# The same two-layer decoder with its long-lived SBUF tiles at other addresses

## The chip, the cores and the metric

The kernel runs on one core of a Trainium2 chip. The metric is the device time of one execution in microseconds (us); a lower time is better. The time before is the median of three runs, 2254.27 us (2254.26 to 2255.32).

## The reference, cut to what matters

Two layers over 256 tokens of width 2048, all in fp32. Layer 0 mixes tokens with forgetting attention (16 heads of 128), layer 1 with sliding-window attention (32 query heads, 4 key heads of 64, with sinks and rotary positions). Each mixer is followed by a gated feed-forward part of width 5632 with a causal convolution of width 3. Shift, scale and gate of every sub-layer come from a conditioning vector `c`.

```python
for i in range(DEPTH):
    mod = c_act @ ada_w[i] + ada_b[i]
    sh1, sc1, g1, sh2, sc2, g2 = jnp.split(mod[:, None, :], 6, axis=-1)
    h = x * (1.0 + sc1) + sh1
    y = fox_attention(h, ...) if i % 2 == 0 else swa_attention(h, ...)
    x = layer_norm(DEEPNORM_ALPHA * x + (1.0 + g1) * y, ln_mix_g[i], ln_mix_b[i])
    h = x * (1.0 + sc2) + sh2
    u = causal_conv3(h @ w_up) + conv_b
    y = (silu(u[..., :D_FF]) * u[..., D_FF:]) @ w_down
    x = layer_norm(DEEPNORM_ALPHA * x + (1.0 + g2) * y, ln_ffn_g[i], ln_ffn_b[i])
```

Weights dominate: about 600 MB of fp32 are read once from HBM.

## The kernel before, in words

**Arithmetic.** To keep fp32 precision with fast matmuls, every operand is split into a high and a low part of type fp32r, and a product is made of three: high times high, high times low, low times high. ScalarE casts a weight tile `w` to its high part `wh` (L276), VectorE subtracts to get the low part `wl` (L287). All matmuls go through the helper `mm`, so they all carry line 76.

**A step.** `stream` (L268) loads a weight tile of two 128-row blocks by 512 columns (512 KB), and one step uses it. There are three kinds of step.

- `w_stationary` (L342), the up-projection of the feed-forward part: the weights are stationary. Eight matmuls have a 128x128 block of `wh` stationary and stream 512 columns of `hHL` past it (high and low halves of the input, side by side); then eight have a block of `wl` stationary and stream the 256 columns of the high half. Their outputs are called `wd`, and the four blocks of 128 features go round four PSUM banks. 16 matmuls a step.
- `x_mm` (L298), with the input stationary: 128x128 blocks of the input stay, and 512 columns of `wh` or `wl` stream past. The input is `hHL` (fox values, all projections of layer 1; outputs `xs`), `gT` (the down-projection) or `oT` (the attention output). 12 matmuls a step, each of 512 columns. In the output projection the first 12 of the 16 blocks of `oT` lie in tiles of the pool `gp`; the last four are put into `hHL`, which is free by then (`o_tile`, L727).
- `w_mm` (L325), for query and key of layer 0 (outputs `ws`): weights stationary, 256 columns of `hHL` streaming. 24 matmuls a step.

**Order.** SP issues the loads, ten weight tiles ahead; `wh` and `wl` have four buffers each, so ScalarE and VectorE prepare up to four steps ahead of TensorE. Beside this VectorE sums the conditioning matrix row by row into `acc` (L406, `ada_vector`), paced by rates that were set by hand for each stage; transposes of `x` for the next modulation (L469, L508) and the short matmuls that turn `acc` into columns (output `sm`) are slipped in between two steps. `hHL` is written once for each sub-layer by `mod_pair` (L473). `gate` holds the row that scales a sub-layer's output (L621).

**Addresses.** A tile is a range of bytes that is the same in each partition. The pool `cst`, with one buffer for each name, lays its tiles out in the order in which the program first asks for them, each rounded up to 32 bytes, from byte 1152. The pools `wp` (`w`), `hl` (`wh`, `wl`) and `gp` (`gT`, `oT`, `qT` and others) follow; `wp` begins at byte 77312, which is 151 x 512, and all tiles of these three pools begin at multiples of 512 bytes. A [128, 24] tile named `gap`, 96 bytes that nothing uses, fills up `cst` to that point.

Of the kernel before, what the change touches and what calls it, by code (L numbers as in the profile page):

```python
# [10 lines left out]
F32 = mybir.dt.float32  # L11
F32R = mybir.dt.float32r
# [5 lines left out]
P = 128  # L18
D = 2048
S = 256  # L20
NT = S // P
KC = D // P
DEPTH = 2
FH = 16
FW = 2048
SQ = 32
# [15 lines left out]
def hybrid_trunk(ctx: ExitStack, tc: tile.TileContext, a: dict, out: bass.AP):  # L42
# [6 lines left out]
    cst = ctx.enter_context(tc.tile_pool(name="cst", bufs=1))  # L49
# [16 lines left out]
    def bank(name="sm"):  # L66
        return psp.tile([P, 512], F32, tag="ps", name=name)
# [10 lines left out]
    def pin(ins, on=True):  # L78

        if on:  # L80
            tc.keep_in_program_order(ins)
# [14 lines left out]
    adab = a["ada_b"].rearrange("l (r p) -> l r p", p=P)  # L96
    nc.sync.dma_start(rows0[:NADA, 1, :], adab[0])

    ident = cst.tile([P, P], F32, name="ident")
    nc.gpsimd.memset(ident, 0.0)  # L100
    nc.gpsimd.affine_select(out=ident, in_=ident, compare_op=ALU.not_equal, fill=1.0, base=0,
# [2 lines left out]
    nc.gpsimd.memset(ones, 1.0)  # L104

    mask = cst.tile([P, 3, P], F32, name="mask")
    nc.gpsimd.memset(mask, 0.0)
    nc.gpsimd.affine_select(out=mask[:, 1, :], in_=mask[:, 1, :], compare_op=ALU.is_gt, fill=NEG, base=0,
                            pattern=[[1, P]], channel_multiplier=-1)
    nc.gpsimd.affine_select(out=mask[:, 2, :], in_=mask[:, 2, :], compare_op=ALU.is_ge, fill=NEG, base=0,  # L110
                            pattern=[[-1, P]], channel_multiplier=1)

    sel = cst.tile([P, 2, FH], F32, name="sel")
    nc.gpsimd.memset(sel, 0.0)
    for j, bases in enumerate(((64, 96), (0, 32))):
        for b in bases:
            nc.gpsimd.affine_select(out=sel[:, j, :], in_=sel[:, j, :], compare_op=ALU.not_equal,
                                    fill=1.0, base=-b, pattern=[[-1, FH]], channel_multiplier=1)

    x = cst.tile([P, NT, D], F32, name="x")  # L120
    csil = cst.tile([KC, P], F32, name="csil")
    nc.scalar.activation(csil, rows0[:KC, 0, :], AF.Silu)
    cact = cst.tile([P, KC], F32, name="cact")
# [9 lines left out]
    HR = ROPE_DIM // 2  # L133
    lcol = cst.tile([P, 4, DEPTH, KC], F32, name="lcol")
    ccol = cst.tile([P, DEPTH, CW + 1, NF], F32, name="ccol")
    sink = cst.tile([P, SQ], F32, name="sink")
    nsink = cst.tile([P, SQ], F32, name="nsink")
    sint = cst.tile([P, NT, HR], F32, name="sint")
    cost = cst.tile([P, NT, HR], F32, name="cost")

# [29 lines left out]
    def rotary():  # L170

        nc.gpsimd.dma_start(sink, a["swa_sinks"][0].partition_broadcast(P))
        posr = cst.tile([NT, P], I32, name="posr")
        nc.gpsimd.dma_start(posr, a["positions"].rearrange("b (t p) -> (b t) p", p=P))
        yield
        pin(nc.vector.tensor_scalar_mul(nsink, sink, -1.0))
        posf = cst.tile([NT, P], F32, name="posf")
        pin(nc.vector.tensor_copy(posf, posr))
        yield
        pt = bank()  # L180
        nc.tensor.transpose(pt[:, :NT], posf, ident[:NT, :NT])
        yield
        posc = cst.tile([P, NT], F32, name="posc")
        nc.vector.tensor_copy(posc, pt[:, :NT])
        inv = [float(np.float32(ROPE_THETA ** (-2.0 * i / ROPE_DIM))) for i in range(HR)]
        ang = cst.tile([P, NT, HR], F32, name="ang")
        for i in range(HR):
            nc.vector.tensor_scalar_mul(ang[:, :, i], posc, inv[i])
        nturn = cst.tile([P, NT, HR], F32, name="nturn")
        nint = cst.tile([P, NT, HR], I32, name="nint")  # L190
        nc.vector.tensor_scalar_mul(nturn, ang, 1.0 / (2.0 * math.pi))
        nc.vector.tensor_copy(nint, nturn)
        nc.vector.tensor_copy(nturn, nint)
        c1 = 6.28125
        c2 = float(np.float32(np.floor((2 * math.pi - c1) * 2 ** 21) / 2 ** 21))
        c3 = 2 * math.pi - c1 - c2
        for cc in (c1, c2, c3):
            nc.vector.scalar_tensor_tensor(ang, nturn, -cc, ang, op0=ALU.mult, op1=ALU.add)
        PI = float(np.nextafter(np.float32(math.pi), np.float32(0)))
        nc.vector.tensor_scalar(ang, ang, PI, -PI, op0=ALU.min, op1=ALU.max)  # L200
        nc.vector.scalar_tensor_tensor(nturn, ang, -1.0, ang, op0=ALU.mult, op1=ALU.max)
        nc.vector.tensor_scalar(nturn, nturn, -1.0, 0.5 * math.pi, op0=ALU.mult, op1=ALU.add)
        yield
        nc.scalar.activation(sint, ang, AF.Sin)
        nc.scalar.activation(cost, nturn, AF.Sin)
# [249 lines left out]
            print("caught up", l, v, n)  # L455


    hHL = cst.tile([P, KC, 2, S], F32R, name="hHL")
    hH, hL = hHL[:, :, 0, :], hHL[:, :, 1, :]
    cst.tile([P, 24], F32, name="gap")  # L460

    def mod_turn(k, n=1):

# [298 lines left out]
    def fox(l, j):  # L762
# [156 lines left out]
        settle()  # L919
        forget_split()  # L920
        later([forget(), columns(), rotary(), scaled()])
        for blk, rate in zip(range(4), (1.0, 1.3, 1.5, 1.6)):
            then(lambda rate=rate: ada.update(rate=rate))
# [252 lines left out]
```

## Time and profile before

| | |
|---|---|
| median of three runs | 2254.27 us |
| the profiled execution's own time | 2256.26 us |
| its span, first to last instruction | 2254.5 us |
| TensorE busy (PE) | 2203.2 us, 98% |
| weight loads (PEld) | 1892.9 us, 84% |
| VectorE busy (DVE) | 1852.2 us, 82% |
| ScalarE busy (ACT) | 1193.7 us, 53% |
| granted TensorE clock, mean | 0.996 |

PE counts a matmul from its start to a modelled end, and matmuls overlap, so a PE that is busy all the time may still start its matmuls at a faster or slower rhythm. The rhythm can be read from the timeline, where matmuls of one kind are merged into a row with the time of the first start and their count: the start of the next row, less the start of this one, divided by the count, is the distance from one matmul to the next.

### The profile page before, as it was taken

The numbers are of one execution on the slowest core, as the hardware profiler recorded it, in microseconds if no ns is written. First come the engines' busy times: TensorE is split into PE (matmuls) and PEld (weight loads), VectorE is DVE, ScalarE is ACT, GpSimd is POOL, SyncE is SP. The second block draws the span as 40 slices with busy tenths as digits, with TensorE's granted clock in tenths as the row PEclk, the third lists the DMA queues.
The fourth block names the chain that finished last, engine by engine and source line by source line (L and its number), as shares of the span: only waits on it lengthen the run. The fifth ranks groups of instructions, "written<-read, shape, count | busy, mean of one in ns | idle before, by whom it ended". The sixth has DMA issues, their size and how long they took to land. (4 is left out here: it accounts for less than half of the span.)

```text
span 2254.5 us, 33348 instructions
## 1 busy us (share of the span) xinstructions
PE 2203.2 (98%) x12196; PEld 1892.9 (84%) x12196; DVE 1852.2 (82%) x2685; ACT 1193.7 (53%) x1873; POOL 19.9 (1%) x51
## 2 busy tenths in 40 slices
PE   7999999999999999999999999999999999999997
PEld 6988898788888888888887788888888888888886
DVE  7989998889988968978978989889988655676766
ACT  4546544356555433555534578646655533555542
POOL 0000000000000000000000000000000000000000
PEclk9999999999999999999999999999999999999999
DMA  9999999869978889878887867678887556666553
GB/s 345 393 372 311 341 379 355 305 222 307 313 243 273 316 292 333 287 226 285 280 307 261 288 202 262 219 254 290 285 268 242 187 194 190 190 192 189 189 194 111
DMA packets 287285, 602.68 MB, mean 267 GB/s; under 512 B 21830, under 2 KB 55304, under 8 KB 286608
## 3 DMA queue, kind: packets, MB, share of 16 engines
q1 hardware_dynamic: 286064, 595.86, 77.8%
q0 software_dynamic: 1056, 4.69, 0.6%
q8 instruction: 95, 1.56, 0.3%
q14 instruction: 70, 0.57, 0.1%
HBM read 598.37 MB, written 2.10 MB: 266 GB/s over the span
## 5 line engine op out<-in xcount | busy, mean ns | idle before, releaser
L276 ACT CAST wh<-w 128x1024 fp32r<-128x1024 f32 x728 | 764.7, 1051 | 802.0 <-PE wd L76 267.5
L287 DVE TENSOR_TENSOR wl<-w,wh 128x1024 fp32r<-128x1024 f32 x728 | 887.0, 1221 | 297.0 <-ACT wh L276 283.7
L76 PE MATMUL wd<-hHL,wh 128*128 128x512 f32 x2816 | 717.9, 397 | 1.1 <-DVE hHL L482 1.1
L76 PEld LDWEIGHTS wd<-hHL,wh 128*128 128x128 f32 x2816 | 503.4, 188 | 100.1 <-issue 2.9
L76 PEld LDWEIGHTS wd<-hHL,wl 128*128 128x128 f32 x2816 | 373.3, 188 | 32.8 <-DVE wl L287 1.6
L76 PE MATMUL wd<-hHL,wl 128*128 128x256 f32 x2816 | 379.6, 277 | 1.1 <-DVE wl L287 1.1
L406 DVE SCALAR_TENSOR_TENSOR acc<-wa,cact,acc 128x1024 f32<-128x1024 f32 x300 | 380.2, 1277 | 0.0
L76 PE MATMUL xs<-wh,gT 128*128 128x512 f32 x1408 | 349.7, 390 | 0.0
L76 PEld LDWEIGHTS xs<-wh,gT 128*128 128x128 f32 x1408 | 263.4, 188 | 54.2
L76 PE MATMUL xs<-wl,gT 128*128 128x512 f32 x704 | 189.3, 389 | 0.0
L76 PE MATMUL xs<-wh,hHL 128*128 128x512 f32 x704 | 185.5, 400 | 2.9 <-DVE hHL L86 2.7
L76 PEld LDWEIGHTS xs<-wl,gT 128*128 128x128 f32 x704 | 132.1, 188 | 27.6
L76 PEld LDWEIGHTS xs<-wh,hHL 128*128 128x128 f32 x704 | 128.9, 190 | 29.1 <-DVE hHL L86 3.5
L76 PE MATMUL ws<-hHL,wh 128*128 128x256 f32 x1024 | 133.2, 282 | 7.1 <-ACT wh L276 4.7
L1066 ACT ACTIVATE u<-s,ccol 128x256 f32<-128x256 f32 x176 | 104.6, 599 | 66.5 <-DVE s L1061 48.8
L76 PEld LDWEIGHTS ws<-hHL,wh 128*128 128x128 f32 x1024 | 125.1, 190 | 11.0 <-ACT wh L276 6.2
L76 PE MATMUL xs<-wh,oT 128*128 128x512 f32 x384 | 99.8, 398 | 0.1
L76 PE MATMUL xs<-wl,hHL 128*128 128x512 f32 x352 | 97.0, 395 | 1.5 <-DVE wl L287 1.5
L551 DVE SCALAR_TENSOR_TENSOR oacc<-wo,cact,oacc 128x512 f32<-128x512 f32 x111 | 79.5, 746 | 15.1 <-DMA wo<-in_ada_w_dram 10.0
L1067 DVE SCALAR_TENSOR_TENSOR u<-s,ccol,u 128x255 f32<-128x255 f32 x176 | 84.0, 479 | 5.6 <-ACT u L1066 5.6
L1069 DVE SCALAR_TENSOR_TENSOR u<-s,ccol,u 128x254 f32<-128x254 f32 x176 | 83.8, 477 | 1.1
L76 PEld LDWEIGHTS xs<-wh,oT 128*128 128x128 f32 x384 | 70.7, 190 | 14.3 <-ACT pT L719 0.5
(223 smaller groups left out, 1643.1 us busy)
## 6 DMA issues: line engine op xcount, KB each, us to landing
w<-in_ffn_w_up_dram SPq DMA_DIRECT2D x352, 512.0 KB, 4.6
wa<-in_ada_w_dram SPq DMA_DIRECT2D x320, 512.0 KB, 5.1
w<-in_ffn_w_down_dram SPq DMA_DIRECT2D x176, 512.0 KB, 4.2
w<-in_fox_w_in_dram SPq DMA_DIRECT2D x96, 512.0 KB, 6.6
wo<-in_ada_w_dram SPq DMA_DIRECT2D x128, 256.0 KB, 6.7
w<-in_swa_w_in_dram SPq DMA_DIRECT2D x40, 512.0 KB, 5.4
w<-in_fox_w_o_dram SPq DMA_DIRECT2D x32, 512.0 KB, 5.8
w<-in_swa_w_o_dram SPq DMA_DIRECT2D x32, 512.0 KB, 5.4
```

Source lines behind the costliest of these rows:

```text
L76: return nc.tensor.matmul(o, lhsT, rhs, start=start, stop=stop, **kw)
L276: pin(nc.scalar.copy(h, w), False)
L287: pin(nc.vector.tensor_tensor(l, w, f32(h), op=ALU.subtract), go in behind)
L406: pin(nc.vector.scalar_tensor_tensor(ac, wo, cact[:, k:k + 1], ac, op0=ALU.mult, op1=ALU.add), True)
L551: nc.vector.scalar_tensor_tensor(ac, wk, cact[:, kc:kc + 1], ac, op0=ALU.mult, op1=ALU.add)
L1066: nc.scalar.activation(u, s, AF.Identity, bias=cw(CW, f), scale=cw(2, f))
L1067: nc.vector.scalar_tensor_tensor(u[:, 1:], s[:, :S - 1], cw(1, f), u[:, 1:], op0=ALU.mult, op1=ALU.add)
L1069: nc.vector.scalar_tensor_tensor(u[:, 2:], s[:, :S - 2], cw(0, f), u[:, 2:], op0=ALU.mult, op1=ALU.add)
```

## The change

No instruction is added, removed or reordered in the program text; only the places where `cst` tiles are first asked for move, and with that their addresses. `sel`, `sink` and `nsink` (128 bytes each) come first and fill the 384 bytes from 1152 to 1536. `hHL` and `x` are declared right behind `mask`, and a first tile for each of the names `acc` and `gate` is declared there, unused, so that the later tiles of these names get its place. `gap` moves behind `posc`.

| tile | bytes a partition | start before | mod 512 | start after | mod 512 |
|---|---|---|---|---|---|
| ident, ones | 512 each | 1152, 1664 | 128 | 1536, 2048 | 0 |
| mask | 1536 | 2176 | 128 | 2560 | 0 |
| hHL | 32768 | 25280 | 192 | 4096 | 0 |
| x | 16384 | 3840 | 256 | 36864 | 0 |
| acc | 8192 | 59552 | 160 | 53248 | 0 |
| gate | 8192 | 67744 | 160 | 61440 | 0 |
| A0 | 1024 | 58368 | 0 | 74656 | 416 |
| ccol | 2816 | 22080 | 64 | 71488 | 320 |
| pool wp | | 77312 | 0 | 77312 | 0 |

The starts after are worked out from the sizes in the new order; the sum of the sizes is the same, so the pools behind `cst` stay where they were.

```diff
+    sel = cst.tile([P, 2, FH], F32, name="sel")
+    sink = cst.tile([P, SQ], F32, name="sink")
+    nsink = cst.tile([P, SQ], F32, name="nsink")
     ident = cst.tile([P, P], F32, name="ident")
...
     mask = cst.tile([P, 3, P], F32, name="mask")
+    hHL = cst.tile([P, KC, 2, S], F32R, name="hHL")
+    x = cst.tile([P, NT, D], F32, name="x")
+    for tag in ("acc", "gate"):
+        cst.tile([P, D], F32, tag=tag, name=tag)
...
-    sel = cst.tile([P, 2, FH], F32, name="sel")
...
-    x = cst.tile([P, NT, D], F32, name="x")
...
-    sink = cst.tile([P, SQ], F32, name="sink")
-    nsink = cst.tile([P, SQ], F32, name="nsink")
...
         posc = cst.tile([P, NT], F32, name="posc")
+        cst.tile([P, 24], F32, name="gap")
...
-    hHL = cst.tile([P, KC, 2, S], F32R, name="hHL")
     hH, hL = hHL[:, :, 0, :], hHL[:, :, 1, :]
-    cst.tile([P, 24], F32, name="gap")
```

## The prediction, made before the change was run

> **What bounds the kernel now.** I read the page first, then the stages by windows, then the waits inside a stage, and last the timeline, for the rhythm of the matmuls.
>
> ```profile
> span 2254.5 us, 33348 instructions
> PE 2203.2 (98%) x12196; PEld 1892.9 (84%) x12196; DVE 1852.2 (82%) x2685; ACT 1193.7 (53%) x1873; POOL 19.9 (1%) x51
> PEclk9999999999999999999999999999999999999999
> ```
>
> TensorE is busy for 98% of the span at the full granted clock, so a gain has to come from matmuls that follow each other faster. By stages (columns: length, then busy time and count of PE, PEld, DVE, ACT and POOL, clock, DMA share, GB/s):
>
> ```profile
> 204.00:357.00 153.00, 148.60 (x1042) 135.78 (x1041) 147.94 (x215) 85.96 (x166) 0.56 (x1) 1.00 0.97 355
> 472.00:747.00 275.00, 273.57 (x1569) 236.24 (x1570) 251.41 (x357) 158.97 (x243) 0.00 (x0) 1.00 0.84 280
> 881.00:1107.00 226.00, 225.99 (x1315) 197.12 (x1314) 191.72 (x265) 124.84 (x189) 0.00 (x0) 1.00 0.83 272
> 1220.00:1380.00 160.00, 155.71 (x788) 127.21 (x786) 145.92 (x305) 111.03 (x247) 2.81 (x7) 1.00 0.72 237
> 1505.00:1780.00 275.00, 273.85 (x1570) 236.22 (x1571) 238.20 (x344) 158.52 (x242) 0.00 (x0) 1.00 0.78 257
> 1910.00:2132.00 222.00, 222.00 (x1282) 193.36 (x1281) 152.64 (x224) 123.77 (x189) 0.00 (x0) 1.00 0.64 190
> ```
>
> The first row is the end of fox attention's projections, where the DMA engines are 97% busy. The second, third, fifth and sixth are the four stretches of up-projection, 998 us together. TensorE fills them; VectorE follows at 91% in the first and 69% in the last. The fourth is layer 1's projections. In the first up-projection stretch the largest waits are
>
> ```profile
> ACT wh L276 <- PE wd L76: 81.7, 67, 2.3
> DVE wl L287 <- ACT wh L276: 21.0, 19, 1.9
> ```
>
> so the chain that prepares the weights stands still because TensorE has not yet given a `wh` buffer back. The preparation is ahead; TensorE sets the time there.
>
> **The change, part by part: hHL as the moving operand.** Two steps of the up-projection, and two of the down-projection, where nothing is in `hHL` and both operands lie at multiples of 512:
>
> ```profile
> 1990.77 2.02 PE L76 MATMUL wd<-hHL,wh 128*128 128x512 f32 x8
> 1992.63 1.07 PE L76 MATMUL wd<-hHL,wl 128*128 128x256 f32 x8
> 1993.55 2.02 PE L76 MATMUL wd<-hHL,wh 128*128 128x512 f32 x8
> ...
> 1996.32 2.02 PE L76 MATMUL wd<-hHL,wh 128*128 128x512 f32 x8
> ```
>
> ```profile
> 1839.62 1.98 PE L76 MATMUL xs<-wh,gT 128*128 128x512 f32 x8
> 1841.43 1.07 PE L76 MATMUL xs<-wl,gT 128*128 128x512 f32 x4
> ...
> 1845.06 1.98 PE L76 MATMUL xs<-wh,gT 128*128 128x512 f32 x8
> ```
>
> The down-projection starts 24 matmuls of 512 columns in 1845.06 - 1839.62 = 5.44 us, one each 0.2267 us. The up-projection needs 1.86 us for eight of the same width (1990.77 to 1992.63), 0.2325 us each, and its two steps take 5.55 us, 2.775 us a step. Those of 256 columns run as fast as they do anywhere: query and key of layer 0 start 24 in 2.72 us, 0.1133 us each, half of 0.2267.
>
> ```profile
> 296.40 1.98 PE L76 MATMUL ws<-hHL,wh 128*128 128x256 f32 x16
> ...
> 299.12 1.07 PE L76 MATMUL ws<-hHL,wh 128*128 128x256 f32 x8
> ```
>
> I take it that the 512-column stream from `hHL`, at 192 above a multiple of 512, is what costs the difference. At a multiple of 512 a step would take 8 x 0.2267 + 8 x 0.1133 = 2.72 us, 0.055 us less. There are 2816 / 8 = 352 such steps:
>
> ```profile
> L76 PE MATMUL wd<-hHL,wh 128*128 128x512 f32 x2816 | 717.9, 397 | 1.1 <-DVE hHL L482 1.1
> L76 PE MATMUL wd<-hHL,wl 128*128 128x256 f32 x2816 | 379.6, 277 | 1.1 <-DVE wl L287 1.1
> L76 PE MATMUL xs<-wh,hHL 128*128 128x512 f32 x704 | 185.5, 400 | 2.9 <-DVE hHL L86 2.7
> L76 PE MATMUL xs<-wl,hHL 128*128 128x512 f32 x352 | 97.0, 395 | 1.5 <-DVE wl L287 1.5
> L76 PE MATMUL xs<-wh,gT 128*128 128x512 f32 x1408 | 349.7, 390 | 0.0
> ```
>
> 352 x 0.055 = **19.4 us**. What could eat it: VectorE's 251.41 us of work in the first stretch does not shrink; with 96 steps 5.3 us shorter it would be 251.4 / 269.7 = 93% busy, still below TensorE, and the 81.7 us that ScalarE waits there are the reserve. So I count the whole.
>
> **hHL as the stationary operand.** In the output projection the same code takes its stationary blocks first from `hHL` and then from `oT`, and nothing else changes:
>
> ```profile
> 1446.87 2.00 PE L76 MATMUL xs<-wl,hHL 128*128 128x512 f32 x8
> 1448.71 1.99 PE L76 MATMUL xs<-wh,hHL 128*128 128x512 f32 x8
> 1450.54 1.08 PE L76 MATMUL xs<-wl,hHL 128*128 128x512 f32 x4
> 1451.45 2.00 PE L76 MATMUL xs<-wh,oT 128*128 128x512 f32 x8
> ...
> 1454.20 1.98 PE L76 MATMUL xs<-wh,oT 128*128 128x512 f32 x8
> 1456.01 1.07 PE L76 MATMUL xs<-wl,oT 128*128 128x512 f32 x4
> ```
>
> From `hHL`, 20 matmuls in 4.58 us, 0.2290 each; from `oT` at multiples of 512, eight in 1.81 us, 0.2263. This is the nearest thing in the trace to the change itself, and the reason why I believe in addresses at all. 704 + 352 = 1056 such matmuls, 0.0023 us each (against 0.2267), make 2.4 us. The 384 of them in the fox values (4 blocks, 8 steps of 12) lie where the DMA engines are 97% busy, so I count half of their 0.9 us: **2.0 us**.
>
> [...]
>
> **Where it will not work fully.** Even at multiples of 512 the rhythm is slower for a while after other matmuls came in between:
>
> ```profile
> 815.77 2.09 PE L76 MATMUL xs<-wh,gT 128*128 128x512 f32 x8
> 817.71 1.09 PE L76 MATMUL xs<-wl,gT 128*128 128x512 f32 x4
> 818.63 0.95 PE L76 MATMUL sm<-ones,acc 128*128 128x1 f32 x8
> ```
>
> The four start 0.230 us apart (0.92 / 4). The four up-projection windows hold 1569 + 1315 + 1570 + 1282 = 5736 matmuls, 5632 of them `wd`; the other 104, in groups of two to eight, break some 30 steps. There I count 8 x 0.0025 = 0.02 us of gain instead of 0.055: **1.0 us** less.
>
> **The other tiles.** I price them at nothing. VectorE's work on `acc` and `x`:
>
> ```profile
> L551 DVE SCALAR_TENSOR_TENSOR oacc<-wo,cact,oacc 128x512 f32<-128x512 f32 x111 | 79.5, 746 | 15.1 <-DMA wo<-in_ada_w_dram 10.0 <-ACT oacc L555 4.3 <-DVE oacc L551 0.4
> L1147 DVE SCALAR_TENSOR_TENSOR x<-x,mv,ln 128x512 f32<-128x512 f32 x8 | 5.7, 744 | 0.0
> ```
>
> The same operation takes 746 ns on a tile at 160 above a multiple of 512 and 744 ns at 256 above, so addresses do not matter to VectorE by more than 2 ns in 746; `A0` and `ccol`, which move to odd offsets, are read by ScalarE and VectorE in the shadow of TensorE. At the same 0.3%, VectorE's 1852 us would move by at most 5 us either way, under that shadow.
>
> Sum: 19.4 + 2.0 - 1.0 = 20.4 us. The profiled execution would go from 2256.26 to 2235.9 (its span from 2254.5 to 2234.1). The median of the runs lies 2.0 us below that execution, so I forecast **2234 us**.
>
> **The rivals.**
>
> *Only half a remedy (2246 us).* Each up-projection step changes between 512 and 256 columns, and each such change may count as a break as above; then all 352 steps gain 0.02 us, 7.0 us, and the stationary part 2.0 to bring it down 9 us, or 2245 to 2246. For it: the slow rhythm after breaks. Against it: layer 0's query and key alternate `wh` and `wl` at a steady 0.1133.
>
> *Another cause (2252 us).* The up-projection alone changes its PSUM bank with each matmul. If that costs the 0.0058 us, only the stationary 2.0 us are won. Against it: the 256-column matmuls change banks as often and lose nothing, though the time of their weight loads could hide it. A step further is the reading that starts never matter, which gives 2254 us: the rows of `hHL` and `oT` would then have to differ by chance, and the same holds if the tiles do not land where I worked out. [...]
>
> *Slower (2264 us).* With `hHL` at a multiple of 512, the moving stream and the next weight load, which starts with it, run through the same offsets at the same time. In the 256-column matmuls the loads leave no room, and a collision would show. A slow rhythm for these exists:
>
> ```profile
> 228.22 1.10 PE L76 MATMUL ws<-hHL,wl 128*128 128x256 f32 x8
> 229.16 0.81 PE L76 MATMUL o<-pT,v 128*128 128x256 f32 x4
> ```
>
> 0.94 / 8 = 0.1175 us instead of 0.1133. On the 2816 `wl` matmuls of the up-projection that is 11.8 us; if the `wh` half gains nothing for the same reason, 2254.3 + 11.8 - 2.0 = 2264. It decides from 2.0 / 2816 = 0.7 ns a matmul if the `wh` half stays as it is, and from 20.4 / 2816 = 7.2 ns if that gains in full. Against it: in the down-projection both operands lie at multiples of 512 and do not collide.
>
> **How the numbers follow.** Forecast 0.64, half a remedy 0.13, another cause 0.10, no effect 0.05, slower 0.08. A difference under 0.2% (4.5 us) cannot be told from none here. Faster: 0.64 + 0.13 = 0.77; the same: 0.15; slower: 0.08. The low end is the forecast with nothing lost: 19.4 + 2.4 us, and 2 us for the runs' spread and matmuls after breaks that gain more, 2230. The high end takes in half a remedy and the stationary part alone, 2252.
>
> **What would show it.** The timeline of the up-projection: eight `wd<-hHL,wh` in 1.81 us instead of 1.86, a step in 2.72; with the mean of that group near the 390 ns that the aligned groups show, instead of 397. The output projection's `hHL` rows at 0.2267. The four up-projection stretches shorter by 5.3, 4.4, 5.3 and 4.4 us, the down-projections unchanged. If the `wd<-hHL,wh` rows still start 0.2325 us apart, my reading of the cause is wrong; if they speed up while the stretch does not shorten, VectorE or the loads took it.

## The result and the profile after

The changed kernel is **slower** by 0.4%: 2263.75 us (2262.71 to 2264.56) against 2255.3 us (2254.26 to 2256.72) for the kernel before, a ratio of 1.0036 with a 95% interval of 1.0026 to 1.0047. The forecast was 2234 us. The head of the page of the changed kernel, and its groups that answer to those shown of before:

```profile
span 2262.7 us, 33348 instructions
PE 2212.2 (98%) x12196; PEld 1911.9 (84%) x12196; DVE 1853.1 (82%) x2685; ACT 1193.8 (53%) x1873; POOL 19.9 (1%) x51
...
L76 PE MATMUL wd<-hHL,wh 128*128 128x512 f32 x2816 | 710.6, 394 | 1.1 <-DVE hHL L484 1.1
...
L76 PE MATMUL wd<-hHL,wl 128*128 128x256 f32 x2816 | 393.7, 283 | 1.1 <-DVE wl L291 1.1
```

The span grew by 8.2 us, and PE's busy time by 9.0. The 512-column matmuls on `hHL` did become shorter (397 to 394 ns), but the 256-column ones became longer (277 to 283 ns). Two steps of the last up-projection in the timeline show it without modelled ends:

```profile
1992.33 2.00 PE L76 MATMUL wd<-hHL,wh 128*128 128x512 f32 x8
1994.17 1.11 PE L76 MATMUL wd<-hHL,wl 128*128 128x256 f32 x8
1995.12 2.00 PE L76 MATMUL wd<-hHL,wh 128*128 128x512 f32 x8
```

Eight `wh` matmuls take 1.84 us instead of 1.86, eight `wl` matmuls 0.95 instead of 0.92, the step 2.79 instead of 2.775. The spacings in ns, from each matmul's start to the next, the commonest value at each place in the step, worked out from the starts in both traces:

```
                 wh (512 columns)                  wl (256 columns)
before  226 236 231 236 231 236 231 236   118 113 113 113 113 113 113 113
after   233 236 228 232 231 227 227 227   113 119 120 120 120 120 120 120
```

The `wh` row does end at the 227 ns that was forecast, but only from the sixth matmul on; the `wl` row goes the other way and stays there. By stretches of up-projection (the columns of the prediction's windows), each window laid within 0.3 us of the first and the last `wd` matmul, before and then after:

```profile
472.20:746.90 274.70, 273.47 (x1568) 236.14 (x1569) 251.21 (x357) 158.67 (x243) 0.00 (x0) 1.00 0.84 280
881.10:1107.00 225.90, 225.89 (x1314) 197.06 (x1313) 191.67 (x265) 124.74 (x189) 0.00 (x0) 1.00 0.83 272
1505.00:1779.70 274.70, 273.55 (x1568) 235.97 (x1569) 238.20 (x344) 158.22 (x242) 0.00 (x0) 1.00 0.78 257
1910.10:2132.10 222.00, 222.00 (x1281) 193.39 (x1280) 152.62 (x224) 123.77 (x189) 0.00 (x0) 1.00 0.64 190
```

```profile
474.00:750.40 276.40, 275.23 (x1568) 239.96 (x1569) 251.44 (x357) 158.44 (x242) 0.00 (x0) 1.00 0.83 278
884.60:1112.00 227.40, 227.40 (x1313) 200.31 (x1312) 191.88 (x265) 124.86 (x189) 0.00 (x0) 1.00 0.82 271
1509.80:1786.30 276.50, 275.32 (x1568) 239.89 (x1569) 238.49 (x344) 158.25 (x242) 0.00 (x0) 1.00 0.79 255
1916.70:2140.30 223.60, 223.60 (x1282) 196.75 (x1281) 152.71 (x224) 123.60 (x189) 0.00 (x0) 1.00 0.63 189
```

These stretches grew from 997.3 to 1003.9 us, 6.6 of the 8.2. VectorE's and ScalarE's work is the same; the time went into TensorE's own rhythm. Another 1.7 us came before the first of them (its first matmul starts at 474.2 instead of 472.5), where query and key of layer 0 are matmuls of 256 columns too:

```profile
292.12 2.08 PE L76 MATMUL ws<-hHL,wh 128*128 128x256 f32 x16
...
295.00 2.08 PE L76 MATMUL ws<-hHL,wh 128*128 128x256 f32 x16
```

Here 24 matmuls take 2.88 us, 0.1200 each; it was 0.1133. On all 1536 of them that would be 10 us; most of it does not show, and the stage is the one where the DMA engines were near 100% busy (in the changed kernel a share of 1.02 from 25 to 204 us and of 0.97 from there to 357). That the 1.7 us are the rest of it is likely but not shown: over the kernels below that move `hHL` alone, the first up-projection starts anywhere between 473.0 and 475.8 us. The part that went as forecast is `hHL` as the stationary operand, in the output projection of layer 1:

```profile
1453.65 1.98 PE L76 MATMUL xs<-wh,hHL 128*128 128x512 f32 x8
1455.46 1.07 PE L76 MATMUL xs<-wl,hHL 128*128 128x512 f32 x4
1456.37 1.98 PE L76 MATMUL xs<-wh,oT 128*128 128x512 f32 x8
```

12 matmuls in 2.72 us, 0.2267 each instead of 0.2290. That is worth little in time: layer 1's projections (`xs<-wh,hHL` and `xs<-wl,hHL`, 480 matmuls) go from 153.9 to 153.7 us, with transposes and waits in between.

### The profile page after: what moved, and what is told of

Its sections match the earlier page's. It is cut to its first block, busy times and chain, and to the rows that moved or that the text cites. A ratio compares the mean times of both kernels' runs of the same rounds, so it can differ in the third digit from the quotient of the medians.

```text
span 2262.7 us, 33348 instructions
## 1 busy us (share of the span) xinstructions
PE 2212.2 (98%) x12196; PEld 1911.9 (84%) x12196; DVE 1853.1 (82%) x2685; ACT 1193.8 (53%) x1873; POOL 19.9 (1%) x51
## 5 line engine op out<-in xcount | busy, mean ns | idle before, releaser
L291 DVE TENSOR_TENSOR wl<-w,wh 128x1024 fp32r<-128x1024 f32 x728 | 886.8, 1220 | 303.1 <-ACT wh L280 294.5
L76 PE MATMUL wd<-hHL,wh 128*128 128x512 f32 x2816 | 710.6, 394 | 1.1 <-DVE hHL L484 1.1
L76 PEld LDWEIGHTS wd<-hHL,wl 128*128 128x128 f32 x2816 | 383.5, 190 | 28.5 <-DVE wl L291 1.6
L76 PE MATMUL wd<-hHL,wl 128*128 128x256 f32 x2816 | 393.7, 283 | 1.1 <-DVE wl L291 1.1
```

The source lines that it names most:

```text
L76: return nc.tensor.matmul(o, lhsT, rhs, start=start, stop=stop, **kw)
L291: pin(nc.vector.tensor_tensor(l, w, f32(h), op=ALU.subtract), go in behind)
```

## The experiments

All kernels keep every instruction unless the text says otherwise. "Distance" is the start of the moving operand less that of the stationary one, modulo 256 bytes; the time from one matmul's start to the next is called spacing.

**Is it hHL alone?** One kernel moves nothing but `hHL` in the old layout, the other moves `hHL` alone back in the new one. The spare tiles around `hHL` add up to 512 bytes, so the places of all other tiles modulo 512 stay.

```diff
 # old layout, hHL at 25600
+    cst.tile([P, 80], F32, name="lead")
     hHL = cst.tile([P, KC, 2, S], F32R, name="hHL")
+    cst.tile([P, 48], F32, name="trail")
 # new layout, hHL at 4096 + o (o = 64, 128, 160, 192, 224, 256)
+    cst.tile([P, o // 4], F32, name="lead")
     hHL = cst.tile([P, KC, 2, S], F32R, name="hHL")
+    cst.tile([P, (512 - o) // 4], F32, name="trail")
```

> The layout of before with hHL alone at a multiple of 512 bytes (25600); x, acc, gate and the constants keep their place modulo 512. If hHL's start alone decides, as a reader of the matmuls' rhythms must think: 2263.5 us, wl matmuls of 256 columns 0.1195 us apart, wh matmuls of 512 columns about 0.230. If the other tiles carry the loss: 2255 us, and rhythms of 0.1133 and 0.2325.

> The new layout with hHL alone back at 192 above a multiple of 512 (4288); x, acc, gate and the constants stay at multiples of 512. If hHL's start alone decides: 2255 us, rhythms of 0.1133 (256 columns) and 0.2325 (512 columns) as before. If the other tiles carry the loss: 2263.5 us. If hHL's distance from the start of SBUF matters rather than its remainder: something else than both.

`hHL` alone at a multiple of 512: 2264.93 us, ratio 1.0038 (1.0025 to 1.0051). `hHL` alone back at 192: 2256.28 us, ratio 1.0001 (0.9992 to 1.0011). The whole effect of the change is the place of `hHL`; `x`, `acc`, `gate` and the constants gave nothing that can be measured. Nor does it matter how far `hHL` lies from the start of SBUF: at 25600 the up-projections take 1003.9 us as at 4096, and at 4288 997.4 us, against 997.3 at 25280.

**How does it depend on the place?**

> The new layout with hHL at 128 above a multiple of 512. If a collision of the moving read with the weight load that starts beside it needs equal starts, the 256-column matmuls are back at 0.1133; 512 columns then at 0.2325 as at 192 (2255 us) or, if they follow the offset too, between 0.2267 and 0.2325 (2236 to 2255 us). If any multiple of 128 collides: about 2264 us.

> The new layout with hHL at 256 above a multiple of 512. If the collision repeats each 256 bytes, this is as at 0: 2264 us, 256 columns at 0.1195. If it repeats each 512 bytes: 256 columns at 0.1133 and 2236 to 2255 us, by what the 512-column matmuls do.

> hHL at 64 above a multiple of 512, all else at multiples of 512. At 0 and 256 the rhythms were equal, so the pattern repeats each 256 bytes. If it is the size of the distance that counts, 64 above is like 64 below (192): 2255 us, 0.2325 and 0.1133. If the direction counts, the collision of the 256-column matmuls stays (0.1195) and the time is 2262 to 2270 us.

> hHL at 160 above a multiple of 512, between 128 (2270 us) and 192 (2256 us). If whole blocks of 64 bytes count, as at 128: 2270 us. If the stall shrinks with the distance: about 2263 us.

> hHL at 224 above a multiple of 512, between 192 (2256 us, 256 columns without collision, 512 columns with one) and 256 (2264 us, the reverse). If whole blocks of 64 bytes count, as at 192: 2256 us. If starts between blocks free both kinds: 2236 us. If they trouble both: 2275 us.

What came out, with the median over steps of the time that the eight `wh` and the eight `wl` matmuls take (ns), and the sum of the four up-projection stretches:

| hHL modulo 512 | wh | wl | up-projections, us | time, us | ratio to before (95%) |
|---|---|---|---|---|---|
| 0 (the change) | 1841 | 953 | 1003.9 | 2263.75 | 1.0036 (1.0026 to 1.0047) |
| 64 | 1834 | 907 or 943 | 992.1 | 2252.99 | 0.9986 (0.9977 to 0.9995) |
| 128 | 1866 | 954 | 1009.6 | 2270.26 | 1.0065 (1.0050 to 1.0080) |
| 160 | 1870 | 937 | 1009.7 | 2272.32 | 1.0072 (1.0057 to 1.0087) |
| 192 (as before) | 1862 | 912 | 997.4 | 2256.28 | 1.0001 (0.9992 to 1.0011) |
| 224 | 1862 | 952 | 1010.7 | 2271.37 | 1.0070 (1.0055 to 1.0085) |
| 256 | 1841 | 953 | 1004.0 | 2264.70 | 1.0037 (1.0023 to 1.0052) |

256 gives the rhythms of 0, so the pattern seems to repeat each 256 bytes; the next run gives a second pair. The two kinds of matmul want different places: 512 columns do best at 0 and 64, 256 columns at 192 and, in every other step, at 64. 128, 160 and 224 are the worst and cannot be told apart by their times. 64 wins a little; the place of the kernel before was the second best, and a multiple of 512 loses to both. For 128 every guess was too low (at most 2264 us). The guess that 64 above is like 64 below missed by 2 us to the good, and its rhythms are not those of 192; the guess of 2262 to 2270 for the other case missed by more. For 256 the first guess was right, for 160 the first was near, for 224 the third was nearest.

**Is it hHL's own place, or its distance from the weights?** The pools of the weights and of `gT` and `oT` move by 64 bytes while `hHL` stays at a multiple of 512.

```diff
-        cst.tile([P, 24], F32, name="gap")
+        cst.tile([P, 40], F32, name="gap")
```

> The changed layout with hHL, x, acc, gate and the constants at multiples of 512, and the pools of w, wh, wl, gT and oT 64 bytes further on, so that hHL begins 192 above them modulo 256, as in the kernel before. If the distance between the two operands' starts decides: 2255 us, with 512 columns at 0.2325 and 256 at 0.1133, and the down-projection, whose two operands moved together, unchanged at 0.2267. If hHL's own start decides: 2264 us with the rhythms of the changed kernel.

```profile
1997.57 1.07 PE L76 MATMUL wd<-hHL,wl 128*128 128x256 f32 x8
1998.48 2.02 PE L76 MATMUL wd<-hHL,wh 128*128 128x512 f32 x8
2000.34 1.07 PE L76 MATMUL wd<-hHL,wl 128*128 128x256 f32 x8
2001.26 2.02 PE L76 MATMUL wd<-hHL,wh 128*128 128x512 f32 x8
```

The rhythms of the kernel before are back (1.86 and 0.92 us for eight), the up-projections take 997.6 us, and the down-projections, whose operands moved together, 486.8 us against 486.9 before. All this with `hHL` at a multiple of 512. So it is the distance between the two operands that counts; and since it is 448 modulo 512 here and was 192 before, this is the second pair 256 bytes apart with the same rhythms. The swapped roles agree. Where `hHL` is stationary and `wh` streams (`xs<-wh,hHL`), `hHL` at 192 makes a distance of 64, and eight matmuls take 1835 ns in the median; `hHL` at 64 makes a distance of 192, and they take 1867. In the up-projection, where `hHL` streams, the distances of 64 and 192 give 1834 and 1862.

The time was 2265.32 us all the same (ratio 1.0045, 1.0029 to 1.0062): the opening lost 8 us, which the forecast did not have. That got a run of its own:

```diff
-        cst.tile([P, 24], F32, name="gap")
+        cst.tile([P, 40], F32, name="gap")
             w = wtile()
...
+            if not pads:
+                pads.append(wp.tile([P, 112], F32, tag="pad", bufs=1, name="pad"))
             h = hl.tile([P, 2, WB], F32R, tag="wh", name="wh")
```

> The changed layout with the ten tiles that the weight loads write (w) alone 64 bytes further on; wh, wl, gT, oT and hHL stay. If loads to such places are slower where the DMA engines are the limit, as the shifted pools suggested: the opening up to the first up-projection 8 us longer, 2272 us, the rest as in the changed kernel. If that loss came from the shifted gT, oT or wh: 2264 us.

2272.4 us, ratio 1.0072 (1.0057 to 1.0087). The first up-projection starts at 482.4 us instead of 474.2, and the four together take 1004.0 us, as in the changed kernel. The first 179 us of the changed kernel's projections and of this one, by windows (the last three columns are the granted clock, the DMA share and GB/s):

```profile
25.00:204.00 179.00, 173.29 (x1279) 163.74 (x1280) 154.88 (x217) 95.76 (x121) 7.25 (x15) 1.00 1.02 365
```

```profile
25.00:204.00 179.00, 167.07 (x1201) 156.72 (x1202) 147.84 (x199) 91.83 (x113) 5.61 (x12) 0.98 1.03 353
```

The DMA engines are as busy and move 353 instead of 365 GB/s. ScalarE's waits for the loads of `fox_w_in` grow from 39.1 to 56.0 us in this window, while its cast of a `w` tile (1049 and 1046 ns) and VectorE's subtraction (1219 and 1220 ns) keep their time, so it is the loads and not their readers that became slower. TensorE's clock is a little lower (0.98), but TensorE is also less busy, 167.07 instead of 173.29 us, so it waits. The loss is made once: the last up-projection ends 8.0 us later than in the changed kernel. So in these runs the place where a load lands matters where the DMA engines are the limit, and not behind that.

**Can both kinds have what they want?** The four `wl` tiles alone move by 64 bytes.

```diff
+            if not pads:
+                pads.append(hl.tile([P, 16], F32, tag="pad", bufs=1, name="pad"))
             l = hl.tile([P, 2, WB], F32R, tag="wl", name="wl")
+            if len(pads) == 1:
+                pads.append(hl.tile([P, 112], F32, tag="pad2", bufs=1, name="pad2"))
```

> The changed layout (hHL, w, wh, gT, oT at multiples of 512) with the four wl tiles alone 64 bytes further on. Theory: a matmul's rhythm depends on where its moving operand starts against the stationary operand that is loaded meanwhile, modulo 256 bytes; 512-column matmuls are free at a distance of 0 and pay a little at 64, 256-column matmuls are free at 192. Then wd<-hHL,wh stays near 0.2267 (distance 0), wd<-hHL,wl goes to 0.1133 (distance 192), a step of the up-projection takes 2.72 us, and xs<-wl,gT goes from 0.2267 to 0.2293 (distance 64): 352 x 0.055 = 19.4 us won and some 3 us lost, 2240 us (2238 to 2246). If the change between the two kinds costs a slow start each step, as the first five wd<-hHL,wh of a step in the changed kernel show: 2250 us. Rival, that the start of hHL alone decides: 2264 us.

2269.28 us, ratio 1.0059 (1.0046 to 1.0072), against forecasts of 2240 and 2250. The theory as it stood fell here. A step of the up-projection:

```profile
1990.98 2.00 PE L76 MATMUL wd<-hHL,wh 128*128 128x512 f32 x8
1992.82 1.11 PE L76 MATMUL wd<-hHL,wl 128*128 128x256 f32 x8
1993.76 2.00 PE L76 MATMUL wd<-hHL,wh 128*128 128x512 f32 x8
```

The `wl` matmuls have `hHL` at 0 and `wl` at 64, as with the shifted pools, and yet they take 0.94 / 8 = 0.1175 us and not 0.114. What differs from the shifted pools is the series in front of them, and this trace has a place that tests it. Between 985 and 1007 us `sm` matmuls come in ahead of four `wh` series and change their rhythm; the `wl` series behind each of the four, at the same addresses as all others, takes 0.91 us in place of 0.94. One of them:

```profile
996.82 0.94 PE L76 MATMUL sm<-ones,acc 128*128 128x1 f32 x8
997.63 2.10 PE L76 MATMUL wd<-hHL,wh 128*128 128x512 f32 x8
999.57 1.07 PE L76 MATMUL wd<-hHL,wl 128*128 128x256 f32 x8
1000.47 1.55 PE L76 MATMUL wd<-hHL,wh 128*128 128x512 f32 x6
```

The down-projection suffered as well (496.0 us for its four stretches instead of 487):

```profile
1848.44 1.10 PE L76 MATMUL xs<-wl,gT 128*128 128x512 f32 x4
1849.37 2.00 PE L76 MATMUL xs<-wh,gT 128*128 128x512 f32 x8
1851.21 1.10 PE L76 MATMUL xs<-wl,gT 128*128 128x512 f32 x4
```

There the four matmuls of the `wl` series, now at another distance, take 0.93 us instead of 0.91, and the eight of the `wh` series behind it, of which the distance had not changed, 1.84 instead of 1.81.

**Does one series set the phase of the next?** With `hHL` at 64 the `wl` series is fast and slow by turns, at the same addresses. The timeline of that kernel:

```profile
1991.79 2.00 PE L76 MATMUL wd<-hHL,wh 128*128 128x512 f32 x8
1993.62 1.07 PE L76 MATMUL wd<-hHL,wl 128*128 128x256 f32 x8
1994.53 1.99 PE L76 MATMUL wd<-hHL,wh 128*128 128x512 f32 x8
1996.36 1.11 PE L76 MATMUL wd<-hHL,wl 128*128 128x256 f32 x8
1997.30 2.00 PE L76 MATMUL wd<-hHL,wh 128*128 128x512 f32 x8
```

0.91 us for eight `wl` in one step, 0.94 in the next, for all of the last 78 steps. The `wh` spacings run 226, 229, 232 over and over; eight is not a multiple of three. Over the whole trace, all 154 complete `wl` series behind a `wh` series whose last spacing is 231 or 232 ns are fast, and all 172 behind another last spacing are slow. The next run leaves out two of a step's eight `wh` matmuls:

```diff
-            for i, f in cells:
+            for i, f in cells[:6]:
                 mm(ps[f], h[:, i, f * P:(f + 1) * P], hHL[:, kc + i].rearrange("p a s -> p (a s)"),
```

> hHL at 64, and only the first six of a step's eight wh matmuls are issued (two of the products are left out, so a step is shorter by about 0.46 us). With hHL at 64 the wl matmuls run at 0.1133 in one step and at 0.118 in the next, at the same addresses, while the wh matmuls repeat 0.226, 0.229, 0.232 in threes. If the rhythm of a series depends on the phase in which the series before it ends, six matmuls, twice three, bring each step into the same phase: the alternation is gone and all wl series of the last up-projection run alike. If the alternation comes from the buffers or the steps themselves, it stays.

```profile
1850.66 1.54 PE L76 MATMUL wd<-hHL,wh 128*128 128x512 f32 x6
1852.04 1.07 PE L76 MATMUL wd<-hHL,wl 128*128 128x256 f32 x8
1852.94 1.54 PE L76 MATMUL wd<-hHL,wh 128*128 128x512 f32 x6
1854.32 1.07 PE L76 MATMUL wd<-hHL,wl 128*128 128x256 f32 x8
1855.22 1.07 PE L76 MATMUL wd<-hHL,wh 128*128 128x512 f32 x4
```

The alternation is gone: 0.90 us for each `wl` series, and 0.113 a matmul in all of the last 78 steps. The addresses, the buffers and the `wl` matmuls are the same as in the kernel with eight. In the three earlier stretches, where VectorE is now the limit (busy for 245.2 of 246.4 us in the first) and TensorE has to wait, fast and slow `wl` series still both occur. So the rhythm of a series depends on the distance of its operands and on the series before it. "Phase" is a name for what the one hands to the other; no view shows it directly. The total of 2120.58 us says nothing here, as this kernel does less work.

**A layout from these readings.** `hHL` gets 192 bytes more, and three views of it start at different places (`v == 3` is the input of a feed-forward part).

```diff
+    hraw = cst.tile([P, KC * 2 * S + 48], F32R, name="hHL")
...
+    def place(b):
+        nonlocal hHL, hH, hL
+        hHL = hraw[:, b // 4:b // 4 + KC * 2 * S].rearrange("p (k a s) -> p k a s", k=KC, a=2)
+        hH, hL = hHL[:, :, 0, :], hHL[:, :, 1, :]
+    place(192)
...
         ada["held"] = False
+        place(64 if v == 3 else 0)
         modulate(*merged(l, v, g, b, ll), normalise)
```

> The changed layout with 192 more bytes for hHL and three views of it: the input of fox attention begins at 192 above a multiple of 512, that of both feed-forward parts at 64, that of layer 1's attention at 0. If the rhythms found at these starts belong to the distance and not to the kernel around them: fox as in the kernel before (first up-projection from 472 us), the up-projections as with hHL at 64 (5 us less than before in all), layer 1's xs<-wh,hHL at 0.227 to 0.230 instead of 0.229 to 0.234: 2249 us (2247 to 2252), ratio to before 0.997. If gains in one stage are lost in another: 2253 to 2256 us.

2250.91 us (2248.18 to 2252.34), ratio 0.9976 (0.9967 to 0.9985): 0.24% faster than the kernel before, and faster than the changed one. Against `hHL` at 64 everywhere (0.9977 to 0.9995) the intervals overlap. By windows, the four up-projection stretches (the row left out is that of layer 1's projections):

```profile
472.00:745.60 273.60, 272.12 (x1568) 237.27 (x1569) 251.43 (x357) 158.96 (x243) 0.00 (x0) 1.00 0.84 281
880.00:1104.60 224.60, 224.55 (x1313) 197.87 (x1312) 191.57 (x265) 124.47 (x189) 0.00 (x0) 1.00 0.83 274
...
1502.20:1775.50 273.30, 272.08 (x1568) 237.13 (x1569) 238.03 (x344) 157.69 (x242) 0.00 (x0) 1.00 0.79 258
1905.90:2126.70 220.80, 220.80 (x1282) 194.37 (x1282) 152.54 (x224) 123.92 (x189) 0.00 (x0) 1.00 0.64 191
```

The up-projections take 992.1 us from the first `wd` matmul on, as with `hHL` at 64 everywhere (997.3 before); the first starts at 472.5 us, as before (474.3 with `hHL` at 64 everywhere). Layer 1's 480 projection matmuls take 153.5 us; the changed kernel has 153.7, and `hHL` at 64 everywhere 154.5. Each stage kept what its start gave it elsewhere, though the differences outside the up-projections are small against the scatter between kernels.

## Why the prediction was wrong

**TensorE as the bound: right.** Both ways, the time followed the matmuls' rhythm. In the first up-projection VectorE's work stayed at 251 us while the stretch went from 274.7 to 276.4, and to 273.3 with the best layout.

**hHL as the stationary operand: right in mechanism.** In unbroken series the matmuls went to 0.2267 us as the rows of `oT` said. The price of 2.0 us was too high: 0.3 us came out in layer 1's projections, which is not clear of noise (the kernel that moves `hHL` alone in the old layout takes 154.2 us there), and none can be seen in layer 0. Of the 67 complete series of eight `xs<-wh,hHL` under 2 us, 22 now take 1820 ns or less, where none did before, but the mean falls by 4 ns alone, from 1855 to 1851: the 26 series behind `xs<-wl,hHL` go from 1834 to 1821, the 41 behind other matmuls stay at 1868 and 1869. The prediction applied its own rule on breaks to the up-projection only.

**hHL as the moving operand: the step that failed.** "At a multiple of 512 a step would take 8 x 0.2267 + 8 x 0.1133 = 2.72 us" has two terms, and both were wrong. The second was the larger error. The 0.1133 us of the 256-column matmuls was taken for their pace "anywhere", but both rows that it came from, `wd<-hHL,wl` and `ws<-hHL,wh`, had the same `hHL` at 192. It held at that distance, and the change gave it away: 953 - 912 = 41 ns a step, 352 x 0.041 = 14.4 us lost where the sum had entered a small gain. The first term, 0.046 us a step (1.86 less 8 x 0.2267), came to 21 ns (1862 to 1841), 7.4 us instead of 16: the `wh` series reaches 227 ns only after five matmuls, each time anew. 14.4 - 7.4 = 7.0 us, against the 6.6 that the four stretches grew.

**The breaks.** The prediction saw that the rhythm is slow after other matmuls and charged 30 steps for it. In the changed kernel the change between `wl` and `wh` series acts like such a break: in 323 of the 345 complete `wh` series the first five spacings are 228 ns or more and the last three 228 or less, most often 227. That was the rival "half a remedy", and its half did happen, 21 ns a step where it had said 20; what it left out is the loss of the `wl` series.

**The rivals.** The one that ended on the other side named the matmuls that slowed down, those of 256 columns when both operands start alike. That a collision with the weight loads is the reason is not shown, and distances of 128, 160 and 224 slow them too (954, 937 and 952 ns for eight, against 912 at 192), where the starts are not alike. Its price, 11.8 us on 0.1175 us a matmul, was too low, and its total of 2264 us met 2263.75 by luck: it also let the `wh` half gain nothing, and its errors cancel. Its chance of 0.08 was too small because of one argument: "in the down-projection both operands lie at multiples of 512 and do not collide". Those are 512-column matmuls; the prediction had no row of 256 columns at a distance of 0 in a steady series, and that should have weighed against the sum. The slow row that it did show (228.22) has `hHL` at 192, where another series of the same kind, from 224.44 to 225.35, takes 0.91 us instead of 0.94: two rhythms at one set of addresses were already in the trace before. "Another cause", the PSUM banks, is out: they change the same way in all kernels of the table, and the last three of a step's `wh` matmuls run at 227 ns in the changed kernel although each changes its bank. The reading that starts never matter is out as well: 2252.99 to 2272.32 us by the place of `hHL` alone.

## What to carry to other kernels

A rate read off one operand is a rate at that operand's address (0.1133 us for a 256-column matmul with `hHL` at 192, 0.1200 with it at a multiple of 512): before an address is moved, ask of every group that reads the tile whether the trace shows that group, at that width, at the new distance. What counts for these fp32r matmuls is the distance between the moving and the stationary operand, modulo 256 bytes as far as it was tried (eight `wh` and eight `wl` matmuls take 1841 and 953 ns at 0 and at 256), together with the series that ran before (907 or 943 ns for eight `wl` at 64), and "aligned" is not the best distance for all of them (953 ns for eight `wl` at 0, 912 at 192); scan multiples of 64 and read the spacing of each kind of matmul, which tell it before the total can. A tile that serves several kinds of matmul can have a view at another start for each (2250.91 us with three views, 2255.77 before).

## What the runs showed of the hardware that was not expected

- Two fp32r operands at equal starts give the shortest spacing seen for 512 columns in a long series (0.2267 us), but for 256 columns one of 0.1200 us, where 0.1133 was seen at a distance of 192.
- At one set of addresses a series has more than one rhythm (0.113 and 0.118 us for 256 columns), and the series in front of it chooses: a `wl` series behind a last `wh` spacing of 231 or 232 ns was fast, one behind 225 to 230 ns slow, in all such cases with `hHL` at 64 and with `wl` at 64. Why the distances of 64 and 192 differ stays open: the runs show when it happens, not what causes it.
- Weight loads that land 64 bytes off a multiple of 512 ran at 353 to 354 GB/s where the DMA engines were the limit (25 to 204 us, a DMA share of 1.03 and 1.04), against 365 in the changed kernel and 368 in the one before, whose loads land at multiples of 512. With the `w` tiles alone moved the first up-projection starts 8.2 us later (482.4 instead of 474.2 us). Why the place where a load lands counts, no run here shows.
